# Forgetting attention: gate bias rows written to DRAM relative to each query block, instead of formed on GpSimd

## The chip, the cores and the metric

One Trainium2 chip, one of its cores. The metric is device time in microseconds, the median of several executions of one launch. The names of the engines in the profile: PE is TensorE's matmul, PEld its weight load, DVE is VectorE, ACT is ScalarE, POOL is GpSimd, SP is SyncE, which here only issues transfers.

## The reference, cut to what matters

The model has two layers over a residual stream of 512 positions by 1024 features. Layer 0 is a dilated-window attention with a gated ConvFFN. Layer 1 is the "forgetting attention" (FoX) with its own ConvFFN. Its keys, values and forget gates come from the stream after layer 0:

```python
kvf = rms_norm(h, kv_norm) @ w_kvf
k_sh = kvf[..., :B_WIDTH].reshape(B, T, B_HEADS, HEAD_DIM)
v_sh = kvf[..., B_WIDTH:2 * B_WIDTH].reshape(B, T, B_HEADS, HEAD_DIM)
log_f = jax.nn.log_sigmoid((kvf[..., 2 * B_WIDTH:] + b_f).astype(jnp.float32))
c_sh = jnp.cumsum(log_f, axis=1)
...
for i in range(T // BLK):            # fox_mixer; BLK = 128, T = 512, 16 heads of 64
    q0, q1 = i * BLK, (i + 1) * BLK
    s = jnp.einsum('bqhd,bkhd->bhqk', q[:, q0:q1], k[:, :q1]).astype(jnp.float32) * scale
    s = s + (c_t[:, :, q0:q1, None] - c_t[:, :, None, :q1])
    causal = jnp.arange(q0, q1)[:, None] >= jnp.arange(q1)[None, :]
    s = jnp.where(causal, s, NEG)
    p = jax.nn.softmax(s, axis=-1).astype(v.dtype)
    outs.append(jnp.einsum('bhqk,bkhd->bqhd', p, v[:, :q1]))
```

The bias of a score is the cumulative gate of the query minus that of the key. A term that is the same for all keys of one query drops out of the softmax. So the bias of a row may be taken against any fixed position: against the query itself, or against the first query of the block.

## The kernel before

All of it runs in float32 on one core. A matrix operand is split into a high part and a remainder, and a product is three matmuls (the helper `mm3`, L283 to L285). Weights arrive through the class `Weights`: a transfer on SyncE's queue brings a piece of 128 by 1024 (L50), ScalarE rounds it to the high part (`high`, L60), and VectorE subtracts to get the remainder (`low`, L78). For some pieces ScalarE writes the negative high part (`minus`, L71) and a transfer from GpSimd's queue adds the raw weight to it (`low_added`, L98). `ahead` and `ahead_dma` say how many pieces are prepared and loaded ahead. Loads, issues and engine instructions stand in each engine's queue in the order in which the source calls them (the schedule is manual). Waits follow from data and from buffers: a tile comes out of a pool and waits for the last use of what lay in its place. The pool `t4` has ten places of 4 KB in each partition; it holds raw weights, the bias tiles, the probabilities, gains and some of the tiles `dsums` (sums of down-projection weights for the next ConvFFN, formed on VectorE at L586 to L589 and written to DRAM from GpSimd's queue at L594).

The stage that the change edits begins after the ConvFFN of layer 0. First come the keys in eight chunks (`keys`, with the remainders at L1446). Beside them the generator `gates` forms the cumulative log gates `c8`, 16 heads by 512 positions, times 8 (L1480, L1481); times 8 because the scores are scaled by 1/8 together with the bias. At chunk 6 `c8` is written to DRAM as `cd` (L1576). After the keys TensorE transposes `c8` into `cq`, which has a column for each query block and head (L1579; copied out of PSUM at L1581). Then come the second half of the values, in four weight steps with the first query projections between them. `load_ck(j)` (L1531) loads the rows of the two heads of pair j from `cd`, repeated over all 128 partitions.

The attention loop runs over 32 units (j, i): head pair j = 0..7, query block i = 0..3, so unit (j, i) has (i + 1) x 128 keys. Its stages are a pipeline over the step n:

- `f_scores`: TensorE, scores of blocks 2 and 3 of pair j and of blocks 0 and 1 of pair j + 1, in the steps with i = 2 (L1630);
- `f_bias`: GpSimd, for unit n + 1 (L1612, L1613, see the diff);
- `f_exp`: VectorE adds scores and bias and takes the row minimum of the negated sum (L1640), ScalarE takes the exponential with its row sum (L1642), for unit n;
- `f_norm`: VectorE, reciprocal (L1650) and scaling of the probabilities in place, one instruction for each head (L1652), for unit n - 1;
- `f_transpose`: TensorE transposes the probabilities of unit n - 2 (L1664), ScalarE copies them out of PSUM (L1666);
- `f_pv`: TensorE, probabilities times values, four units at a time (L1679); `f_out_high` (L1689) and `f_out_low` (L1693) split the output.

Between these stand the query projections of the next pairs (`q_part`, six matmuls each, with `q_high` L1552 and `q_low` L1558) and the first part of the output projection (`acc`) near the end. The query projections run out in pair 6. Weight pieces are prepared in the same loop by `W.high`, `W.low`, `W.minus` and `W.low_added`.

Of the kernel before, what the change touches and what calls it, by code (L numbers as in the profile page):

```python
# [9 lines left out]
F32 = mybir.dt.float32  # L10
# [3 lines left out]
ALU = mybir.AluOpType  # L14

D = 1024
T = 512
# [6 lines left out]
NEG = -1e30  # L24
# [93 lines left out]
def trunk_kernel(ctx, tc, x, norm_gains, w_qkv_a, w_o_a, w_q_b, w_o_b, kv_norm, w_kvf, b_f,  # L118
                 w_up, conv_w, conv_b, w_down, rope, out):
    nc = tc.nc  # L120
    act, dve, pool, pe, sp = nc.scalar, nc.vector, nc.gpsimd, nc.tensor, nc.sync
# [5 lines left out]
    sml = ctx.enter_context(tc.tile_pool(name="sml", bufs=6))  # L127
    psp = ctx.enter_context(tc.tile_pool(name="psp", bufs=8, space=bass.MemoryType.PSUM))

    def t8(shape, dt=F32, name="t8"):  # L130
        return p8.tile(shape, dt, tag="t8", name=name)

    def t4(shape, dt=F32, name="t4"):
        return p4.tile(shape, dt, tag="t4", name=name)

    def t2(shape, dt=F32, name="t2"):
        return p2.tile(shape, dt, tag="t2", name=name)

    def bank(shape, name="bank"):
        return psp.tile(shape, F32, tag="ps", name=name)  # L140
# [114 lines left out]
    ident = cst.tile([128, 128], F32, name="ident")  # L255
# [15 lines left out]
    for s in range(2):  # L271
# [5 lines left out]
                       fill=NEG, base=0, channel_multiplier=-1)  # L277
    pool.affine_select(mask0[:, 128:256], mask0[:, 128:256], pattern=[[-1, 128]], compare_op=ALU.is_ge,
                       fill=NEG, base=0, channel_multiplier=1)
    same = cst.tile([128, 4], F32, name="same")  # L280

    def mm3(o, ah, al, bh, bl, first, last, shared=False):
        pe.matmul(o, ah, bh, start=first, stop=False, skip_group_check=shared)  # L283
        pe.matmul(o, ah, bl, start=False, stop=False, skip_group_check=shared)  # L284
        pe.matmul(o, al, bh, start=False, stop=last, skip_group_check=shared)  # L285
# [78 lines left out]
    def xs(xT, kc, s):  # L364
        return xT[0][kc // 4][:, kc % 4, s], xT[1][kc // 4][:, kc % 4, s]
# [1073 lines left out]
    def keys(c):  # L1439
        o = bank([128, T], name="k_ps")  # L1440
        feat_mm(W.get(), bd2.xT, o, ALL)
        if c % 2 == 0:
            kst[c // 2] = t8([128, 2, 2, T], F32R, name=f"kst{c // 2}")
        k = kst[c // 2][:, c % 2]
        act.copy(k[:, 0], o)
        dve.tensor_tensor(k[:, 1], o, k[:, 0].bitcast(F32), ALU.subtract)  # L1446

    c8 = t2([16, T], name="c8")
# [38 lines left out]
    def values(banks, w, s, blocks):  # L1487
        for b in blocks:
            for k in range(2):
                kc = 2 * s + k  # L1490
                ah, al = xs(bd2.xT, kc, slice(b * 128, b * 128 + 128))
                mm3(banks[b], ah, al, w[0][:, k, :], w[1][:, k, :], kc == 0, kc == KD - 1)

    def value_weight():
        return [t.rearrange("p (k c) -> p k c", k=2) for t in W.get()]

    def keep_values(hf, b, o):
        if hf not in Vt:
            Vt[hf] = t8([128, 4, 512], name=f"Vt{hf}")
        (act.copy if b % 2 else dve.tensor_copy)(Vt[hf][:, b, :], o)  # L1500
# [22 lines left out]
    del wv  # L1523
    next(down1)

    cks = {}

    def load_ck(j):
        t = t4([128, 2, T], name="ck")
        s = cd[2 * j:2 * j + 2, :]  # L1530
        sp.dma_start(t, bass.AP(tensor=s.tensor, offset=s.offset, ap=[[0, 128], [T, 2], [1, T]]))  # L1531
        cks[j] = t

    qT = {}
    qps = {}
# [1 line left out]
    def q_part(j, i):  # L1537

        if j >= 8:
            return  # L1540
        if i == 0:
            qps[j] = (bank([128, T], name="q_ps"), [t.rearrange("p (k c) -> p k c", k=8) for t in W.get()])
        o, (wh, wl) = qps[j]
        for kc in (2 * i, 2 * i + 1):
            bh, bl = xs(xTq, kc, ALL)
            mm3(o, wh[:, kc, :], wl[:, kc, :], bh, bl, kc == 0, kc == KD - 1)

    def q_high(j):
        if j >= 8:
            return  # L1550
        qT[j] = t8([128, 2, T], F32R, name="qst")
        act.copy(qT[j][:, 0], qps[j][0])  # L1552

    def q_low(j):
        if j >= 8:
            return
        o, t = qps.pop(j)[0], qT[j]
        dve.tensor_tensor(t[:, 1], o, t[:, 0].bitcast(F32), ALU.subtract)  # L1558

    cd = tc.dram_tile([16, T], F32, name="cd")  # L1560


    xTq = [], []
    for c in range(8):
        keys(c)
        for kc in range(2 * c, min(2 * c + 2, KD)):
            if kc % 4 == 0:
                for part, name in zip(xTq, ("xqh", "xql")):
                    part.append(t8([128, 4, T], F32R, name=f"{name}{kc // 4}"))
            bd2.second(xTq, kc)  # L1570
        if 1 <= c <= 5:
            next(gate)
        if c in (0, 1):
            next(down1)
        if c == 6:
            sp.dma_start(cd, c8)  # L1576
    cqp = bank([128, 4, 16], name="cq_ps")
    for b in range(4):
        pe.transpose(cqp[:, b, :], c8[:, b * 128:(b + 1) * 128], ident[:16, :16])  # L1579
    cq = sml.tile([128, 4, 16], F32, tag="cq", name="cq", bufs=1)  # L1580
    dve.tensor_copy(cq, cqp)  # L1581


    banks = [bank([128, 512], name="v_ps") for _ in range(4)]
    for s in range(4):
        values(banks, value_weight(), s, range(4))
        next(down1, None)
        if s == 0:
            W.ahead = 2
            q_part(0, 0)  # L1590
            q_part(0, 1)
            load_ck(0)
        elif s == 1:
            q_part(0, 2)
        elif s == 2:
            q_part(0, 3)
            q_high(0)
            q_low(0)
    for b in range(4):
        keep_values(1, b, banks[b])  # L1600


    prob = {}

    bia = {}

    def f_bias(j, i):
        n = (i + 1) * 128
        bias = t4([128, 2, T], name="bias")
        for hh in range(2):  # L1610
            hd = 2 * j + hh
            pool.tensor_scalar(bias[:, hh, :n], cks[j][:, hh, :n], -1.0, cq[:, i, hd:hd + 1], ALU.mult, ALU.add)  # L1612
        pool.affine_select(bias[:, :, n - 128:n], bias[:, :, n - 128:n], pattern=[[0, 2], [-1, 128]],  # L1613
                           compare_op=ALU.is_ge, fill=NEG, base=0, channel_multiplier=1)
        bia[j, i] = bias

    sc = {}

    def f_scores(j, blocks):
        wide = blocks[0] >= 2  # L1620
        if not wide:
            both = [bank([128, 2, 256], name="s_ps") for _ in range(2)]
        k = kst[j // 2][:, j % 2]
        for i in blocks:
            nn = max(256, (i + 1) * 128)
            sc[j, i] = [bank([128, T], name="s_ps") for _ in range(2)] if wide else [o[:, i] for o in both]
            for qp, kp in ((0, 0), (0, 1), (1, 0)):
                for hh in range(2):
                    own = slice(64 * hh, 64 * hh + 64)
                    pe.matmul(sc[j, i][hh][:, :nn], qT[j][own, qp, i * 128:(i + 1) * 128], k[own, kp, :nn],  # L1630
                              start=qp + kp == 0, stop=qp == 1)
# [63 lines left out]
    units = [(j, i) for j in range(8) for i in range(4)]  # L1695
    po = Proj(8, 4, lambda kc: (OTb[kc // 2][:, 0, kc % 2, :], OTb[kc // 2][:, 1, kc % 2, :]))
    wo = W.n_get + 7
    fill = [(kc, b) for b in range(2) for kc in range(4)]
    W.ahead, W.ahead_dma = 1, 1
    for i in range(3):  # L1700
        q_part(1, i)
        if i == 0:
            W.split(W.n_get + 1)
    f_bias(0, 0)
    N = len(units)
    pv_next = 0
    down1 = down_sums([(1, 9), (1, 10)], in_one, pool, 2, 0)
# [12 lines left out]
    for n in range(N + 3):  # L1720
        live = n < N
        if live:
            j, i = units[n]
            if i == 0 and j + 1 < 8:
                load_ck(j + 1)
            if i == 2:
                q_part(j + 2, 1)
                f_scores(j, (2, 3))
                if j + 1 < 8:
                    f_scores(j + 1, (0, 1))  # L1730
                values_of(n)
        if live:
            f_exp(j, i)
        if 1 <= n <= N:
            f_norm(*units[n - 1])
        if live:
            if n + 1 < N:
                f_bias(*units[n + 1])
            if i == 1:
                q_low(j + 1)  # L1740
            if i == 2 and j < 2 or (j, i) >= (6, 2):
                W.low()
            if i == 3 and j:
                f_out_low(j - 1)
            if i != 2:
                q_part(j + 1 + (i > 0), (i + 3) % 4)
            if (j, i) in ((7, 1), (7, 2)):
                next(down1)
        if 2 <= n < N + 2:
            f_transpose(*units[n - 2])  # L1750
        if live and i == 1 and 2 <= j < 6:
            W.minus()
            W.low_added()
        if n >= N + 3 - len(fill):
            po.both(*fill[n - N - 3 + len(fill)])

        if n >= N and n % 4 in (0, 2):
            values_of(n)
        while outs:
            f_out_high(outs.pop())  # L1760
        if live and i == 0:
            q_high(j + 1)
        if live and (i == (j < 2) if j < 6 else (j, i) >= (6, 1) and W.n_split < wo + 4):
            W.high()
# [53 lines left out]
```

## Time and profile before

| what | value |
|---|---|
| time, median of 3 (lowest to highest) | 1107.25 us (1107.01 to 1107.43) |
| time of the profiled execution | 1107.3 us |
| its span in the trace | 1105.5 us |
| busy: TensorE matmul, VectorE, ScalarE, GpSimd | 1095.3, 878.3, 672.3, 213.3 us |
| transfers: bytes, mean rate | 236.26 MB, 214 GB/s |
| GpSimd in the stretch 580 to 722 us: L1612 with 128, 256, 384, 512 keys | 16 each, mean 453, 650, 722, 915 ns |
| GpSimd there: L1613 | 32, mean 439 ns |

The span is the time from the first to the last instruction in the trace; the time of the execution has 1.8 us more around it. Rows of a timeline give the start in microseconds from the begin of the span, the duration (of a run of equal instructions: from the first start to the last end), engine, line, operation, output <- inputs, sizes and count; in brackets stands the idle time of the engine ahead of the row and what ended it. Matmuls overlap, so the duration of a row on TensorE is longer than the step to the next row; the starts are what to compare.

### The profile page before, as it was taken

The page shows a single profiled execution, that of the slowest core. Times are in us where ns is not written, and L with a number is a line of the kernel's source. Part 1 is how long each engine was busy: PE and PEld are TensorE (multiplying, and loading weights), DVE is VectorE, ACT ScalarE, POOL GpSimd, SP SyncE. Part 2 cuts the span into 40 slices and gives each one's busy share as a digit, 9 for nine tenths or more (in the row PEclk, how much of TensorE's full clock was granted, in tenths as well). Part 3 has the DMA queues.
Part 4 walks back from the last instruction along what each step waited for, and adds up shares of the span by engine and source line. Part 5 has one row for each costly group of instructions (what it writes and reads, how often), then busy time and mean ns, then how long its engine had stood idle before and what let it go on. Part 6 is the DMA issues. An engine that isn't in the chain of part 4 may idle for free.

```text
span 1105.5 us, 18058 instructions
## 1 busy us (share of the span) xinstructions
PE 1095.3 (99%) x6609; PEld 951.4 (86%) x6609; DVE 878.3 (79%) x1493; ACT 672.3 (61%) x1116; POOL 213.3 (19%) x309
## 2 busy tenths in 40 slices
PE   9999999999999999999999999999999999999997
PEld 6988889899999988888878788789899999988886
DVE  6697788888788689897686677868888788779894
ACT  7654575756666747576451587746656666647572
POOL 2632001311111211000000546500311111211000
PEclk9999999999999999999999999999999999999999
DMA  9799854477987989794447434684368878979862
GB/s 323 179 367 411 312 170 136 90 184 187 214 191 185 243 264 324 287 322 116 133 153 274 172 108 123 187 267 128 84 179 202 203 186 186 235 265 325 311 248 76
DMA packets 184928, 236.26 MB, mean 214 GB/s; under 512 B 12352, under 2 KB 132152, under 8 KB 184840
## 3 DMA queue, kind: packets, MB, share of 16 engines
q1 hardware_dynamic: 169224, 182.94, 50.9%
q0 software_dynamic: 14944, 52.18, 20.6%
q8 instruction: 52, 0.85, 0.3%
q14 instruction: 36, 0.29, 0.1%
q10 hardware_dynamic: 672, 0.00, 0.0%
HBM read 166.08 MB, written 39.63 MB: 186 GB/s over the span
## 4 chain that ended last, share of the span: by engine, by line
PE 94%; ACT 2%; DVE 1%; DMA 1%; issue 1%; POOL 0%; SPq 0%; DVEq 0%; ACTq 0%; POOLq 0%
PE up L284 13%; PE up L283 13%; PE up L285 13%; PE acc L283 9%; PE acc L285 8%; PE acc L284 8%; PE v_ps L283 2%; PE v_ps L285 2%; PE v_ps L284 2%; PE qk_ps L284 2%; PE qk_ps L283 2%; PE qk_ps L285 2%; PE first L285 1%; PE first L283 1%; PE first L284 1%; PE k_ps L285 1%
## 5 line engine op out<-in xcount | busy, mean ns | idle before, releaser
L283 PE MATMUL acc<-w 128*128 128x512 f32 (+1 forms) x311 | 120.6, 388 | 0.3 <-DVE mix L332 0.3
L285 PE MATMUL acc<-w 128*128 128x512 f32 (+1 forms) x311 | 120.4, 387 | 0.0
L284 PE MATMUL acc<-w 128*128 128x512 f32 (+1 forms) x267 | 103.2, 387 | 0.0
L283 PE MATMUL up<-xsh,w 128*128 128x256 f32 x352 | 99.6, 283 | 0.0
L284 PE MATMUL up<-xsl,w 128*128 128x256 f32 x352 | 99.6, 283 | 0.0
L285 PE MATMUL up<-xsh,w 128*128 128x256 f32 x352 | 99.6, 283 | 0.0
L78 DVE TENSOR_TENSOR w<-wraw,w 128x1024 fp32r<-128x1024 f32 x62 | 82.0, 1339 | 21.6 <-ACT w L60 21.2
L620 ACT ACTIVATE bb<-up,conv 128x512 f32<-128x512 f32 x80 | 59.6, 776 | 58.7 <-DVE up L1007 47.9
L60 ACT CAST w<-wraw 128x1024 fp32r<-128x1024 f32 x82 | 84.3, 1048 | 17.1 <-PE v_ps L284 6.9
L284 PE MATMUL up<-xcl,w 128*128 128x512 f32 (+1 forms) x276 | 93.5, 339 | 0.0
L284 PE MATMUL up<-xbl,w 128*128 128x512 f32 (+1 forms) x276 | 93.5, 339 | 0.0
L283 PE MATMUL up<-xbh,w 128*128 128x512 f32 (+1 forms) x276 | 93.5, 339 | 0.0
L283 PE MATMUL up<-xch,w 128*128 128x512 f32 (+1 forms) x276 | 93.5, 339 | 0.0
L285 PE MATMUL up<-xbh,w 128*128 128x512 f32 (+1 forms) x276 | 93.5, 339 | 0.0
L285 PE MATMUL up<-xch,w 128*128 128x512 f32 (+1 forms) x276 | 93.4, 338 | 0.0
L283 PEld LDWEIGHTS acc<-w 128*128 128x128 f32 x311 | 58.4, 188 | 12.4 <-DVE mix L332 0.7
L285 PEld LDWEIGHTS acc<-w 128*128 128x128 f32 x311 | 58.4, 188 | 12.0
L283 PEld LDWEIGHTS up<-xsh,w 128*128 128x128 f32 x352 | 67.6, 192 | 0.0
L284 PEld LDWEIGHTS up<-xsl,w 128*128 128x128 f32 x352 | 67.6, 192 | 0.0
L285 PEld LDWEIGHTS up<-xsh,w 128*128 128x128 f32 x352 | 67.6, 192 | 0.0
L621 DVE SCALAR_TENSOR_TENSOR bb<-up,conv,bb 128x511 f32<-128x511 f32 x80 | 59.5, 743 | 5.5 <-ACT bb L620 5.5
L623 DVE SCALAR_TENSOR_TENSOR bb<-up,conv,bb 128x510 f32<-128x510 f32 x80 | 59.9, 748 | 2.8
(312 smaller groups left out, 3154.8 us busy)
## 6 DMA issues: line engine op xcount, KB each, us to landing
wraw<-in_w_up_dram SPq DMA_DIRECT2D x88, 512.0 KB, 5.7
w<-wraw POOLq DMA_DIRECT2D x32, 512.0 KB, 6.4
dT<-dsums SPq DMA_DIRECT2D x28, 512.0 KB, 6.6
w<-wsum POOLq DMA_DIRECT2D x24, 512.0 KB, 5.8
dsums<-in_w_down_dram SPq DMA_DIRECT2D x22, 512.0 KB, 7.5
dsums<-in_w_down_dram SPq DMA_DIRECT2D x44, 256.0 KB, 7.5
hD<-hc POOLq DMA_DIRECT2D x44, 256.0 KB, 6.4
dact<-hD SPq DMA_DIRECT2D x44, 256.0 KB, 5.4
```

Source lines behind the costliest of these rows:

```text
L60: self.nc.scalar.copy(pair[:, 0], raw)
L78: self.nc.vector.tensor_tensor(pair[:, 1], raw, pair[:, 0].bitcast(F32), ALU.subtract)
L283: pe.matmul(o, ah, bh, start=first, stop=False, skip_group_check=shared)
L284: pe.matmul(o, ah, bl, start=False, stop=False, skip_group_check=shared)
L285: pe.matmul(o, al, bh, start=False, stop=last, skip_group_check=shared)
L620: act.activation(bb[:, s, :], ps, AF.Identity, bias=cp[:, 3, ch:ch + 1], scale=cp[:, 2, ch:ch + 1])
L621: dve.scalar_tensor_tensor(bb[:, s, 1:], ps[:, :T - 1], cp[:, 1, ch:ch + 1], bb[:, s, 1:], ALU.mult, ALU.add)
L623: dve.scalar_tensor_tensor(bb[:, s, 2:], ps[:, :T - 2], cp[:, 0, ch:ch + 1], bb[:, s, 2:], ALU.mult, ALU.add)
```

## The change

`cd` becomes four arrays of 16 by 512 in DRAM. Array i holds c of the first position of query block i minus c of every position, formed on VectorE as `rel` at key chunk 6, one instruction and one write for each block. The transposes of `c8` and the tile `cq` go. Instead of one load of `c` for each head pair there is one load for each unit, of the first (i + 1) x 128 keys of array i, straight into the unit's bias tile, issued three units ahead. GpSimd's two additions for each unit go; its mask over the last 128 columns (the diagonal block) stays, and now works on the loaded tile.

```diff
-    cks = {}
-
-    def load_ck(j):
-        t = t4([128, 2, T], name="ck")
-        s = cd[2 * j:2 * j + 2, :]
-        sp.dma_start(t, bass.AP(tensor=s.tensor, offset=s.offset, ap=[[0, 128], [T, 2], [1, T]]))
-        cks[j] = t
+    bia = {}
+
+    def load_bias(n):
+        j, i = divmod(n, 4)
+        if j < 8:
+            bia[j, i] = t = t4([128, 2, T], name="bias")
+            m = (i + 1) * 128
+            s = cd[i, 2 * j:2 * j + 2, :m]
+            sp.dma_start(t[:, :, :m], bass.AP(tensor=s.tensor, offset=s.offset, ap=[[0, 128], [T, 2], [1, m]]))
...
-    cd = tc.dram_tile([16, T], F32, name="cd")
+    cd = tc.dram_tile([4, 16, T], F32, name="cd")
...
         if c == 6:
-            sp.dma_start(cd, c8)
-    cqp = bank([128, 4, 16], name="cq_ps")
-    for b in range(4):
-        pe.transpose(cqp[:, b, :], c8[:, b * 128:(b + 1) * 128], ident[:16, :16])
-    cq = sml.tile([128, 4, 16], F32, tag="cq", name="cq", bufs=1)
-    dve.tensor_copy(cq, cqp)
+            for i in range(4):
+                rel = t2([16, T], name="rel")
+                dve.tensor_scalar(rel, c8, -1.0, c8[:, i * 128:i * 128 + 1], ALU.mult, ALU.add)
+                sp.dma_start(cd[i], rel)
...
-            load_ck(0)
+            load_bias(0)
         elif s == 1:
             q_part(0, 2)
+            load_bias(1)
         elif s == 2:
             q_part(0, 3)
             q_high(0)
             q_low(0)
+            load_bias(2)
...
-    def f_bias(j, i):
-        n = (i + 1) * 128
-        bias = t4([128, 2, T], name="bias")
-        for hh in range(2):
-            hd = 2 * j + hh
-            pool.tensor_scalar(bias[:, hh, :n], cks[j][:, hh, :n], -1.0, cq[:, i, hd:hd + 1], ALU.mult, ALU.add)
-        pool.affine_select(bias[:, :, n - 128:n], bias[:, :, n - 128:n], pattern=[[0, 2], [-1, 128]],
-                           compare_op=ALU.is_ge, fill=NEG, base=0, channel_multiplier=1)
-        bia[j, i] = bias
+    def f_mask(j, i):
+        d = bia[j, i][:, :, i * 128:(i + 1) * 128]
+        pool.affine_select(d, d, pattern=[[0, 2], [-1, 128]], compare_op=ALU.is_ge, fill=NEG, base=0,
+                           channel_multiplier=1)
...
-    f_bias(0, 0)
+    f_mask(0, 0)
...
             j, i = units[n]
-            if i == 0 and j + 1 < 8:
-                load_ck(j + 1)
+            load_bias(n + 3)
...
             if n + 1 < N:
-                f_bias(*units[n + 1])
+                f_mask(*units[n + 1])
```

More of the change, by code (lines that the diff above doesn't have):

```diff
@@ L1603, in trunk_kernel @@
     prob = {}
-    bia = {}
-    def f_bias(j, i):
-        n = (i + 1) * 128
-        bias = t4([128, 2, T], name="bias")
-        for hh in range(2):
-            hd = 2 * j + hh
-            pool.tensor_scalar(bias[:, hh, :n], cks[j][:, hh, :n], -1.0, cq[:, i, hd:hd + 1], ALU.mult, ALU.add)
-        pool.affine_select(bias[:, :, n - 128:n], bias[:, :, n - 128:n], pattern=[[0, 2], [-1, 128]],
-                           compare_op=ALU.is_ge, fill=NEG, base=0, channel_multiplier=1)
-        bia[j, i] = bias
+    def f_mask(j, i):
+        d = bia[j, i][:, :, i * 128:(i + 1) * 128]
+        pool.affine_select(d, d, pattern=[[0, 2], [-1, 128]], compare_op=ALU.is_ge, fill=NEG, base=0,
+                           channel_multiplier=1)
     sc = {}
```

## The prediction

> **What bounds the kernel now.** I read the page's busy times first, then TensorE's list of waits, then busy time by stretch over the attention stage that the change edits, then the timelines there, engine by engine.
>
> ```profile
> span 1105.5 us, 18058 instructions
> ...
> PE 1095.3 (99%) x6609; PEld 951.4 (86%) x6609; DVE 878.3 (79%) x1493; ACT 672.3 (61%) x1116; POOL 213.3 (19%) x309
> ```
> ```profile
> PE pT_ps L1664 <- DVE prob L1652: 1.4, 3, 1.1
> ```
> ```profile
> 690.00:700.00 10.00, 9.91 (x92) 7.95 (x90) 8.81 (x32) 8.15 (x23) 8.30 (x17) 1.00 0.79 207
> 700.00:710.00 10.00, 8.66 (x72) 6.83 (x68) 9.45 (x26) 7.66 (x22) 8.38 (x11) 1.00 0.76 264
> ```
>
> The columns of the last view are the stretch, its length, the busy time of TensorE (PE), its weight loads, VectorE (DVE), ScalarE (ACT) and GpSimd (POOL) with their instructions, the granted clock, the share of time in which the transfer engines were busy, and GB/s. TensorE is the bound at full clock (1.00), and its matrix work is not edited. So what the edit can give is what TensorE loses in or near this stage; what it can cost is a new TensorE wait. The list of waits has 1.4 us, but "busy" ends are modelled, so I measure losses by start times instead. First an undisturbed stretch, as a ruler:
>
> ```profile
> 645.18 0.82 PE L1664 MATMUL pT_ps<-ident,prob 128*128 128x128 f32 x6
> 645.76 0.48 PE L283 MATMUL q_ps<-xqh,w 128*128 128x512 f32 x1
> ...
> 647.00 0.39 PE L285 MATMUL q_ps<-xqh,w 128*128 128x512 f32 x1
> 647.23 1.04 PE L1664 MATMUL pT_ps<-ident,prob 128*128 128x128 f32 x8
> 648.02 0.47 PE L283 MATMUL q_ps<-xqh,w 128*128 128x512 f32 x1
> ...
> 649.58 2.21 PE L1630 MATMUL s_ps<-kst,qst 64*128 64x384 f32 x24
> 651.73 0.54 PE L1679 MATMUL o_ps<-pT,Vt 128*64 128x128 f32 x5
> ```
>
> A 512-wide matmul gives way to the next instruction after 0.23 us (647.00 to 647.23), 6 transposes take 0.58, 8 take 0.79 (0.105 per transpose more), 24 score matmuls 2.15. Three places fall behind this ruler; I call them A, B and C:
>
> ```profile
> 631.79 0.40 PE L285 MATMUL q_ps<-xqh,w 128*128 128x512 f32 x1
> 632.36 0.55 PE L1664 MATMUL pT_ps<-ident,prob 128*128 128x128 f32 x3 [0.17 <-DVE prob L1652]
> ...
> 633.39 0.47 PE L283 MATMUL q_ps<-xqh,w 128*128 128x512 f32 x1
> ```
> ```profile
> 694.69 2.14 PE L1664 MATMUL pT_ps<-ident,prob 128*128 128x128 f32 x14
> 696.76 2.62 PE L1630 MATMUL s_ps<-kst,qst 64*128 64x384 f32 x24
> 699.31 0.55 PE L1679 MATMUL o_ps<-pT,Vt 128*64 128x128 f32 x6
> ```
> ```profile
> 705.56 0.40 PE L285 MATMUL acc<-w,OTb 128*128 128x512 f32 x1
> 707.03 0.66 PE L1664 MATMUL pT_ps<-ident,prob 128*128 128x128 f32 x4 [1.07 <-DVE prob L1652]
> 707.96 0.63 PE L1664 MATMUL pT_ps<-ident,prob 128*128 128x128 f32 x4 [0.27 <-ACT pT L1666]
> 708.34 0.47 PE L283 MATMUL acc<-w,OTb 128*128 128x512 f32 x1
> ```
>
> A: 633.39 should have been 631.79 + 0.23 + 0.58 = 632.60, lost 0.79. B: 14 transposes should take 0.79 + 6 x 0.105 = 1.42, with 0.1 to the score matmuls and 2.15 for them, so 698.36 instead of 699.31, lost 0.95. C: 705.56 + 0.23 + 0.79 = 706.58 instead of 708.34, lost 1.76.
>
> **The change, part by part.**
>
> *The four transposes of c (L1579) go.*
>
> ```profile
> 589.00 0.39 PE L285 MATMUL k_ps<-xkh,w 128*128 128x512 f32 x1
> 589.32 0.41 PE L1579 MATMUL cq_ps<-ident,c 16*128 16x16 f32 x4
> ...
> 590.00 0.39 PE L284 MATMUL v_ps<-w,xkh 128*128 128x512 f32 x1
> ```
>
> From 589.00 to the second value matmul at 590.00 are 1.00 us; without the four it is two steps of 0.23. Gain 0.54, on the path itself.
>
> *GpSimd's 64 additions (L1612) go, its 32 masks (L1613) stay.*
>
> ```profile
> L1612 POOL TENSOR_SCALAR bias<-ck,cq x64: 368/688/1914, 618.2 to 707.5; 128x128 f32<-128x128 f32 x16, 128x256 f32<-128x256 f32 x16, 128x384 f32<-128x384 f32 x16, 128x512 f32<-128x512 f32 x16
> ...
> L1613 POOL TENSOR_SCALAR_AFFINE_SELECT bias<-bias x32: 407/408/1274, 619.0 to 709.5; 128x256 f32<-128x256 f32 x32
> ```
> ```profile
> 631.56 1.41 DVE L1652 TENSOR_SCALAR prob<-prob,rl 128x384 f32<-128x384 f32 x2
> ...
> 694.84 1.28 DVE L1652 TENSOR_SCALAR prob<-prob,rl 128x512 f32<-128x512 f32 x2
> ...
> 697.68 0.68 DVE L1558 TENSOR_TENSOR qst<-q_ps,qst 128x512 fp32r<-128x512 f32 x1
> ...
> 713.93 0.75 DVE L1652 TENSOR_SCALAR prob<-prob,rl 128x384 f32<-128x384 f32 x2
> ...
> 716.64 0.88 DVE L1652 TENSOR_SCALAR prob<-prob,rl 128x512 f32<-128x512 f32 x2
> ```
>
> The last two rows come after the last addition (707.5): there VectorE's normalisation of a pair takes 0.75 and 0.88. In A the same shape took 1.41, in B 1.28. I read the difference as VectorE held up by GpSimd. In A the second half would be done at 631.56 + 0.75 = 632.31 instead of 632.97, 0.66 earlier, and the last three transposes wait for just that half: of 0.79 I take 0.66. In B the normalisation would end 0.40 earlier, and the small one behind it and the query subtraction at 697.68, for which the second dozen of score matmuls waits, earlier still; I take 0.93 of 0.95. Bounds for each: 0, if the masks hold VectorE as long, and the whole loss.
>
> C is different:
>
> ```profile
> 705.71 1.06 ACT L60 CAST w<-wraw 128x1024 fp32r<-128x1024 f32 x1
> ...
> 707.43 0.85 ACT L1666 COPY pT<-pT_ps 128x384 f32<-128x384 f32 x2
> ```
>
> TensorE's last four transposes there start at 707.96, as ScalarE's copies end, and ScalarE ran a weight conversion and an exponential right up to those copies. GpSimd does not touch this. Bounds 0 and 1.76; I take 0.25, near the end that ScalarE's rows give.
>
> *Four VectorE rows (rel) and four writes to DRAM in place of one.* They have the shape of the scaling of c:
>
> ```profile
> 582.43 0.41 DVE L1481 TENSOR_SCALAR c<-c 16x512 f32<-16x512 f32 x1
> ...
> 590.04 0.69 DVE L1446 TENSOR_TENSOR kst<-k_ps,kst 128x512 fp32r<-128x512 f32 x1 [3.27 <-ACT kst L1445]
> ```
> ```profile
> 595.45 1.05 ACT L60 CAST w<-wraw 128x1024 fp32r<-128x1024 f32 x1 [4.49 <-PE v_ps L285]
> ```
>
> 4 x 0.41 = 1.64 us, ahead of VectorE's 3.27 us of idle time (586.77 to 590.04), which hides them; without that cover they would cost up to 1.64. The copy of cq (L1581) goes. On SyncE's queue the writes stand ahead of two value weights, dsums loads and a query weight. c was ready at 582.84; rel is ready at the latest by 586.77 + 1.64 = 588.4, so all of these leave up to 5.6 us later. The third value weight is converted at 595.45, and that conversion waited for TensorE to release a buffer, not for the load; I take 0, bound by a 1 us loss.
>
> *32 loads of bias rows in place of 8 of c.* Per head pair 128 partitions x 2 heads x 4 bytes x (128 + 256 + 384 + 512) = 1.31 MB instead of 0.52 MB. Each is issued three units ahead, and a unit lasts some 2.8 us (32 of them in the 618.2 to 707.5 of the L1612 row). Each waits in SyncE's queue for its buffer out of ten: for transposes or exponentials one to three units old. Queued behind are the weights of the next pairs, which in the kernel before waited for the same transposes and exponentials. GpSimd's masks wait for the loads; behind a mask in its queue stand the weight DMAs that accumulate (L98), and VectorE's score additions (L1640) wait for the mask. All this lies beside TensorE: 0, with the loss bounded by the last rival.
>
> Sum against the profiled execution (span 1105.5, time 1107.3): 0.54 + 0.66 + 0.93 + 0.25 = 2.38, so 1104.9. The median, 1107.25, is 0.05 lower, which changes nothing.
>
> **The rivals.**
>
> *The masks hold VectorE too.* For it: 32 masks of 0.41 us stay, one per unit, and the loads free GpSimd to run each early, against any VectorE instruction. Against: a unit has one mask of 0.41 where it had two additions of 0.69 besides. A and B would each give 0.41 less (gain 1.56), or nothing, with C, if each half meets a mask (gain 0.54): 1105.7 to 1106.8. The Trainium skill, page SBUF — State Buffer, section Who interferes with whom, states this as a rule: the second port pair of VectorE is shared with GpSimd and is an exclusive lock, held for the whole instruction by whoever starts first. By that rule the masks still lock; A's 1.41 against 0.75 is what it looks like here.
>
> *C goes too.* For it: its first wait, 1.07, is put down to the stretched normalisation, and VectorE was 9.45 of 10 us busy in that stretch. Against: the copies above. With 1.07 to 1.76 for C in place of 0.25 the gain is 3.2 to 3.9: 1103.4 to 1104.1.
>
> *A weight comes late (slower).*
>
> ```profile
> wraw<-in_w_o_b_dram SPq DMA_DIRECT2D x8, 512.0 KB, 6.2
> ```
> ```profile
> 694.81 6.75 SPq L50 DMA_DIRECT2D wraw<-in_w_o_b_dram  x3
> ```
> ```profile
> 702.87 1.06 ACT L60 CAST w<-wraw 128x1024 fp32r<-128x1024 f32 x1
> ```
>
> In head pair 6 no query projections are left to fill TensorE. The output weight issued at 694.81 is converted on ScalarE at 702.87, 8.06 us later, and landing takes 6.2; ScalarE sets C's end, so a weight later than 8.1 us costs TensorE one for one. The transfer engines are 0.79 busy there, and the bias rows of pairs 6 and 7 now share them. From 8.06 + 2.38 = 10.4 us on the gain is gone; with one weight 5 us late it is 1104.9 + 5 = 1109.9, with two 3 us late each 1110.9. Against it: only 0.13 to 0.4 MB more stands ahead of each weight.
>
> **How the numbers follow.** Forecast 0.50 (own range 1104.3 to 1105.4), masks 0.17, C too 0.20, late weight 0.13. A measurement of this kernel tells some 0.2% (2.2 us) from no change, so the line is at 1105.04: two thirds of the forecast's chance lie below it, all of "C too", none of "masks". Faster 0.33 + 0.20 = 0.53, same 0.17 + 0.17 = 0.34, slower 0.13. The range takes in C too and the masks with the 0.54 alone, and a part of the 1 us by which the third value weight was bounded: 1103.3 to 1107.2; what is left out is most of the late weight's 0.13.
>
> **What would show it.** Value matmuls should follow the key matmuls 0.23 us apart. The longest L1652 pair should fall from 1.28 to 1.41 towards 0.75 to 0.88. A and B should be gone by start times, and C should still start its last transposes as ScalarE's copies end. TensorE should have no wait put down to a bias load or a weight. The forecast is wrong if the stretched pairs stay stretched, if the stage shortens by over 3 us, or if a conversion on ScalarE waits for its load.

## The result and the profile after

| what | before | after |
|---|---|---|
| time, median (lowest to highest), side by side, 14 runs each | 1107.74 us (1106.92 to 1109.31) | 1105.17 us (1104.58 to 1106.94) |
| ratio after to before, 95% interval | | 0.998 (0.9973 to 0.9988) |
| time of the profiled execution, its span | 1107.3, 1105.5 us | 1104.97, 1102.9 us |
| last key matmul to the transposes of the convolution's rows (L566), starts | 136.54 us | 133.84 us |

The change takes 2.57 us from the median, 0.2%. The last row of the table is a ruler for the whole edited stage: it leaves out what differs upstream (the last key matmul starts at 589.00 before and at 589.24 after, with the same TensorE instructions ahead of it). It loses 2.70 us, in one execution of each kernel.

The page of the kernel after, its busy times; then the stretch from 700 to 710 us in the columns of the prediction; then TensorE's list of waits (what waited, for what, us in total, times, longest):

```profile
span 1102.9 us, 18083 instructions
...
PE 1094.1 (99%) x6605; PEld 951.6 (86%) x6605; DVE 873.1 (79%) x1496; ACT 671.5 (61%) x1116; POOL 173.0 (16%) x245
```
```profile
700.00:710.00 10.00, 9.19 (x70) 7.10 (x70) 9.34 (x31) 9.19 (x24) 2.14 (x3) 1.00 0.86 300
```
```profile
PE pT_ps L1659 <- DVE prob L1647: 0.8, 1, 0.8
```

GpSimd is busy 40 us less, VectorE 5; in the stretch of C GpSimd works 2.14 of 10 us in place of 8.38, and the transfer engines 0.86 in place of 0.76. Of TensorE's waits for the normalisation (1.4 in 3 before) one is left, in C. The line numbers have moved by five: the transposes are L1659, the normalisation L1647, the scores L1625, the mask L1609. The same places by start times, kernel after, timeline of TensorE; first the way from keys to values and the end of the ruler:

```profile
589.24 0.39 PE L285 MATMUL k_ps<-xkh,w 128*128 128x512 f32 x1
589.47 0.39 PE L283 MATMUL v_ps<-w,xkh 128*128 128x512 f32 x1
589.70 0.39 PE L284 MATMUL v_ps<-w,xkh 128*128 128x512 f32 x1
...
723.08 0.44 PE L566 MATMUL cv_ps<-ident,cv_rows 44*128 44x44 f32 x4
```

Keys give way to values in two steps of 0.23: 0.46 in place of 1.00. Then A, B and C:

```profile
631.45 0.40 PE L285 MATMUL q_ps<-xqh,w 128*128 128x512 f32 x1
631.70 0.94 PE L1659 MATMUL pT_ps<-ident,prob 128*128 128x128 f32 x6
632.39 0.48 PE L283 MATMUL q_ps<-xqh,w 128*128 128x512 f32 x1
...
693.70 1.69 PE L1659 MATMUL pT_ps<-ident,prob 128*128 128x128 f32 x14
695.32 2.21 PE L1625 MATMUL s_ps<-kst,qst 64*128 64x384 f32 x24
697.46 2.40 PE L1674 MATMUL o_ps<-pT,Vt 128*64 128x128 f32 x40
...
703.80 0.40 PE L285 MATMUL acc<-w,OTb 128*128 128x512 f32 x1
705.01 1.11 PE L1659 MATMUL pT_ps<-ident,prob 128*128 128x128 f32 x8 [0.81 <-DVE prob L1647]
705.88 0.47 PE L283 MATMUL acc<-w,OTb 128*128 128x512 f32 x1
```

By the prediction's ruler A loses 632.39 - 631.45 - 0.81 = 0.13 (0.79 before), B 697.46 - 693.70 - 3.67 = 0.09 (0.95 before), C 705.88 - 703.80 - 1.02 = 1.06 (1.76 before). The gains are 0.66, 0.86 and 0.70; with 0.54 for the transposes of c that is 2.76, against 2.70 by the whole stretch.

Now the instruction that was meant to be held up, first in the kernel before, then after (one line's view: shortest, median and longest in ns, first and last start):

```profile
L1652 DVE TENSOR_SCALAR prob<-prob,rl x64: 280/484/2034, 623.7 to 717.0; 128x128 f32<-128x128 f32 x16, 128x256 f32<-128x256 f32 x16, 128x384 f32<-128x384 f32 x16, 128x512 f32<-128x512 f32 x16
```
```profile
L1647 DVE TENSOR_SCALAR prob<-prob,rl x64: 273/415/505, 623.8 to 714.6; 128x128 f32<-128x128 f32 x16, 128x256 f32<-128x256 f32 x16, 128x384 f32<-128x384 f32 x16, 128x512 f32<-128x512 f32 x16
```
```profile
L1609 POOL TENSOR_SCALAR_AFFINE_SELECT bias<-bias x32: 396/722/1480, 618.4 to 707.2; 128x256 f32<-128x256 f32 x32
```

The longest normalisation falls from 2.03 to 0.51 us. In A the pair took 1.41 and in B 1.28; in the kernel after the same two rows are

```profile
631.22 0.75 DVE L1647 TENSOR_SCALAR prob<-prob,rl 128x384 f32<-128x384 f32 x2
...
693.16 0.88 DVE L1647 TENSOR_SCALAR prob<-prob,rl 128x512 f32<-128x512 f32 x2
```

The median of the masks goes the other way, from 0.41 before to 0.72. That is not one mask taking longer: sixteen of the 32 now run in four groups of four, each behind an adding weight transfer in GpSimd's queue. The rows within a group overlap, and a whole group takes 1.79. Single masks still take 0.41, except a few that ran beside VectorE's weight subtraction; GpSimd's rows, then VectorE's:

```profile
676.19 1.79 POOL L1609 TENSOR_SCALAR_AFFINE_SELECT bias<-bias 128x256 f32<-128x256 f32 x4
...
702.17 1.43 POOL L1609 TENSOR_SCALAR_AFFINE_SELECT bias<-bias 128x256 f32<-128x256 f32 x1 [1.87 <-DVE prob L1647]
```
```profile
702.11 1.22 DVE L78 TENSOR_TENSOR w<-wraw,w 128x1024 fp32r<-128x1024 f32 x1
```

B has a second part, which the prediction did not count. VectorE's row at the head of B, before and after, and GpSimd's row before:

```profile
691.39 0.69 DVE L1640 CUSTOM_DVE_ANT_0 prob<-s_ps,bias 128x512 f32<-128x512 f32 x1 [1.05 <-POOL bias L1613]
```
```profile
688.97 0.69 DVE L1635 CUSTOM_DVE_ANT_0 prob<-s_ps,bias 128x512 f32<-128x512 f32 x1 [0.28 <-POOL bias L1609]
```
```profile
689.19 1.69 POOL L1612 TENSOR_SCALAR bias<-ck,cq 128x512 f32<-128x512 f32 x2
```

Before, VectorE waited 1.05 us there for a mask that stood behind two additions in GpSimd's queue; after, it waits 0.28. From 691.39 on VectorE was busy without a gap until the query subtraction that B waits for, so this late start counts in B beside the stretched normalisations. In A there is no such difference: VectorE's work starts 4.47 us ahead of the query matmul (627.32 to 631.79 before, 626.98 to 631.45 after) in both.

### The profile page after: what moved, and what is told of

The parts are those of the page before. It is cut to its first block, busy times and chain, and to the rows that moved or that the text cites. A ratio compares the mean times of both kernels' runs of the same rounds, so it can differ in the third digit from the quotient of the medians.

```text
span 1102.9 us, 18083 instructions
## 1 busy us (share of the span) xinstructions
PE 1094.1 (99%) x6605; PEld 951.6 (86%) x6605; DVE 873.1 (79%) x1496; ACT 671.5 (61%) x1116; POOL 173.0 (16%) x245
## 4 chain that ended last, share of the span: by engine, by line
PE 97%; DVE 1%; DMA 1%; issue 1%; ACT 0%; DVEq 0%
PE up L285 12%; PE up L284 12%; PE up L283 12%; PE acc L283 9%; PE acc L284 8%; PE acc L285 8%; PE v_ps L285 2%; PE v_ps L283 2%; PE v_ps L284 2%; PE qk_ps L284 2%; PE qk_ps L283 2%; PE qk_ps L285 2%; PE o_ps L1674 2%; PE pT_ps L1659 2%; PE s_ps L1625 2%; PE first L285 1%
```

## The experiments

All times are medians; the ratio is to the kernel before in runs beside it. "Stretch" is the ruler of the table above; A, B, C are us lost by starts in the profiled execution; the last column is the longest single normalisation. Medians that differ by less than 1 us can't be told apart here (every interval is some 2 us wide), so the small terms are read from the starts. These come from one execution of each kernel: low_later lost 0.78 us more than the changed kernel in A and B together, ahead of anything that it moves, so a stretch or a letter alone is no surer than that where no row shows the reason.

| kernel | time, us | ratio (95%) | stretch | A | B | C | longest, us |
|---|---|---|---|---|---|---|---|
| before | 1107.74 | | 136.54 | 0.79 | 0.95 | 1.76 | 2.03 |
| after | 1105.17 | 0.998 (0.9973 to 0.9988) | 133.84 | 0.13 | 0.09 | 1.06 | 0.51 |
| after_again | 1105.21 | 0.9979 (0.9970 to 0.9988) | 134.00 | 0.16 | 0.09 | 1.00 | 0.60 |
| adds_back | 1106.25 | 0.9985 (0.9977 to 0.9994) | 135.68 | 0.95 | 0.61 | 1.65 | 1.37 |
| old_no_gpsimd | 1105.08 | 0.9978 (0.9969 to 0.9986) | 134.48 | 0.03 | 0.16 | 1.22 | 0.49 |
| no_masks_b | 1105.11 | 0.9977 (0.9968 to 0.9987) | 133.82 | 0.03 | 0.09 | 1.16 | 0.49 |
| cq_back | 1105.56 | 0.9978 (0.9969 to 0.9986) | 134.62 | 0.12 | 0.09 | 1.00 | 0.64 |
| norm_first | 1104.80 | 0.9972 (0.9961 to 0.9982) | 133.74 | 0.11 | 0.09 | 0.78 | 0.52 |
| low_later | 1105.39 | 0.9977 (0.9967 to 0.9987) | 135.04 | 0.36 | 0.64 | 1.36 | 0.59 |
| pool_low | 1105.06 | 0.9981 (0.9972 to 0.9990) | 134.18 | 0.12 | 0.09 | 1.25 | 1.74 |
| lead1 | 1104.63 | 0.9971 (0.9959 to 0.9982) | 134.15 | 0.35 | 0.09 | 1.15 | 0.58 |
| rel16 | 1105.41 | 0.9975 (0.9965 to 0.9985) | 134.05 | 0.22 | 0.09 | 0.99 | 0.56 |

### GpSimd's additions, without their data (adds_back)

```diff
     def f_mask(j, i):
+        n = (i + 1) * 128
+        for hh in range(2):
+            pool.tensor_scalar(h[:, i, :n], h[:, i, :n], -1.0, 0.0, ALU.mult, ALU.add)
         d = bia[j, i][:, :, i * 128:(i + 1) * 128]
```

> The changed kernel with 64 additions on GpSimd of the old shapes, two ahead of each mask, on a tile that nothing in the attention reads (its sign is turned twice, so it stays what it was). Theory 1, GpSimd's additions hold VectorE's normalisation whatever they compute: the pairs of the normalisation stretch again (a single one over 1 us, where the changed kernel's longest is 0.505), TensorE loses a part or all of the 2.2 us that A, B and C gave back (0.66 + 0.86 + 0.70), and the run is 0.7 to 2.2 us longer than the changed kernel. Theory 2, the old loss came from VectorE waiting for the additions' result: nobody waits for these, so the normalisation stays at or below 0.505 us and the time is that of the changed kernel within 0.3 us.

The normalisation's line in this kernel, then TensorE in A, B and C, then VectorE in C:

```profile
L1650 DVE TENSOR_SCALAR prob<-prob,rl x64: 275/482/1373, 623.4 to 716.0; 128x128 f32<-128x128 f32 x16, 128x256 f32<-128x256 f32 x16, 128x384 f32<-128x384 f32 x16, 128x512 f32<-128x512 f32 x16
```
```profile
631.76 0.55 PE L1662 MATMUL pT_ps<-ident,prob 128*128 128x128 f32 x3 [0.30 <-DVE prob L1650]
632.54 0.52 PE L1662 MATMUL pT_ps<-ident,prob 128*128 128x128 f32 x3 [0.24 <-DVE prob L1650]
...
694.12 2.15 PE L1662 MATMUL pT_ps<-ident,prob 128*128 128x128 f32 x14
696.20 2.26 PE L1628 MATMUL s_ps<-kst,qst 64*128 64x384 f32 x24
...
706.44 1.11 PE L1662 MATMUL pT_ps<-ident,prob 128*128 128x128 f32 x8 [1.40 <-DVE prob L1650]
```
```profile
703.11 1.66 DVE L78 TENSOR_TENSOR w<-wraw,w 128x1024 fp32r<-128x1024 f32 x1 [0.31 <-ACT w L60]
...
705.90 0.88 DVE L1650 TENSOR_SCALAR prob<-prob,rl 128x512 f32<-128x512 f32 x2
```

Theory 1. No instruction of the attention needs the result of these additions, and still the normalisation has its old median (482 ns against 484), A breaks into two groups of three as before, B's fourteen transposes need 2.08 up to the scores in place of 1.62, and A, B and C together lose 3.21 us, 1.93 more than the changed kernel and near the 3.50 of the kernel before. The stretch is 1.84 longer, the median 1.1 (0.8 if each is taken against the kernel before beside it), with intervals that overlap. It is GpSimd's being at work that costs, not the result of its additions. But the three places don't lose in the same way. In A it is the normalisation (a pair of 1.11 and one of 1.07 ahead of it). In C the pair that TensorE waits for takes 0.88, as in the changed kernel; held is the weight subtraction ahead of it, 1.66 in place of 1.22, beside an addition pair that GpSimd ran from 703.08 to 705.25. In B VectorE waits 0.95 for a mask, which stands behind these additions too, so this kernel does not tell the held normalisation from the late mask.

### GpSimd left out altogether (old_no_gpsimd)

```diff
     def f_bias(j, i):
-        n = (i + 1) * 128
-        bias = t4([128, 2, T], name="bias")
-        for hh in range(2):
-            hd = 2 * j + hh
-            pool.tensor_scalar(bias[:, hh, :n], cks[j][:, hh, :n], -1.0, cq[:, i, hd:hd + 1], ALU.mult, ALU.add)
-        pool.affine_select(bias[:, :, n - 128:n], bias[:, :, n - 128:n], pattern=[[0, 2], [-1, 128]],
-                           compare_op=ALU.is_ge, fill=NEG, base=0, channel_multiplier=1)
-        bia[j, i] = bias
+        bia[j, i] = cks[j]
```

> The kernel before with GpSimd's 64 additions and 32 masks left out: scores get the row of c itself as bias, without mask. Loads, the write and the transposes of c stay as before. Theory 1, A, B and a part of C were GpSimd's alone: they fall to what the changed kernel has (0.13, 0.09, 1.06), 2.2 us less, and the transposes still take 1.00; stretch from the last key matmul to the transposes of the convolution's rows 136.5 - 2.2 = 134.3; time 1.9 to 2.5 below the kernel before and 0.3 to 0.7 above the changed one. Theory 2, the changed kernel's loads cost something that its gains hide: this one comes out at or below the changed kernel in spite of its transposes.

The stretch is 134.48, 2.06 below the kernel before, and the way from keys to values takes 1.00 as there. So 2.06 of the 2.70 us belong to GpSimd's work; 0.54 more are the transposes, and what is left, 0.10, is within the 0.16 by which two executions of the changed kernel differ. Theory 2 finds no support in the stretch. By the median alone (2.88 below the kernel before beside it, and 0.1 below the changed kernel's) theory 2's sign is met: it is lower than theory 1 allowed and doesn't show the 0.5 us that the transposes cost here. Medians don't resolve that, and the stretch is one execution, so the loads' cost is shown to be small and not to be nothing.

### The masks (no_masks, no_masks_b)

```diff
     def f_mask(j, i):
-        d = bia[j, i][:, :, i * 128:(i + 1) * 128]
-        pool.affine_select(d, d, pattern=[[0, 2], [-1, 128]], compare_op=ALU.is_ge, fill=NEG, base=0,
-                           channel_multiplier=1)
+        pass
```

> The changed kernel without GpSimd's 32 masks: the attention sees later positions of its diagonal block too. Theory 1 (the forecast), the masks cost TensorE nothing: A (0.13 lost), B (0.09) and C (1.06) stay within 0.15 each, the normalisations keep their 0.42 us median, time within 0.3 us of the changed kernel. Theory 2 (rival of the prediction), the masks still hold VectorE: C falls by 0.3 to 0.8 and the time by 0.5 to 1.0.

> The changed kernel without GpSimd's 32 masks, once more for its trace: the attention sees later positions of its diagonal block too. Theory 1, the masks cost TensorE nothing: A (0.13), B (0.09) and C (1.06) stay within 0.15 each and the stretch from the last key matmul to the transposes of the convolution's rows stays at 133.8. Theory 2, masks still hold VectorE or come late: the stretch falls by 0.5 to 1.0.

The first of the two had a median of 1104.69 us, ratio 0.9977 (0.9967 to 0.9986); the starts are read from the second. There the stretch is 133.82, against 133.84 and 134.00 with masks; A is 0.03, and C at 1.16 is no better. Theory 1: one mask for each unit costs TensorE nothing that the starts can show, apart from 0.1 in A.

### The transposes of c (cq_back)

```diff
+    cqp = bank([128, 4, 16], name="cq_ps")
+    for b in range(4):
+        pe.transpose(cqp[:, b, :], c8[:, b * 128:(b + 1) * 128], ident[:16, :16])
+    cq = sml.tile([128, 4, 16], F32, tag="cq", name="cq", bufs=1)
+    dve.tensor_copy(cq, cqp)
     banks = [bank([128, 512], name="v_ps") for _ in range(4)]
```

> The changed kernel with the four transposes of c and their copy on VectorE put back between key and value projection; nothing uses their result. Theory 1, they lie on TensorE's path alone: from the last key matmul to the second value matmul 1.00 us again instead of 0.46, everything behind it 0.54 later, time +0.5. Theory 2, the stage behind has slack that takes them up: the start of the transposed stage behind the attention (value of L566) moves by less than 0.2. Theory 3, the additional copy and bank cost VectorE or PSUM more: over 0.8.

TensorE between keys and values in this kernel:

```profile
588.91 0.39 PE L285 MATMUL k_ps<-xkh,w 128*128 128x512 f32 x1
589.23 0.41 PE L1586 MATMUL cq_ps<-ident,c 16*128 16x16 f32 x4
589.57 0.50 PE L283 MATMUL v_ps<-w,xkh 128*128 128x512 f32 x1
589.90 0.39 PE L284 MATMUL v_ps<-w,xkh 128*128 128x512 f32 x1
```

0.99 in place of 0.46, and the stretch is longer by 0.62 to 0.78. They lie on the path; A, B and C stay as they are. The median, 0.4 above the changed kernel (0.1 if each is taken against the kernel before beside it), can't prove it.

### What holds C (norm_first, low_later, pool_low)

In norm_first VectorE normalises unit (6,3) before it adds bias and scores of (7,0).

```diff
+        if n == 28:
+            f_norm(*units[n - 1])
         if live:
             f_exp(j, i)
-        if 1 <= n <= N:
+        if 1 <= n <= N and n != 28:
             f_norm(*units[n - 1])
```

> The changed kernel with one thing moved: at the first unit of pair 7 VectorE normalises (6,3) before it adds bias and scores of (7,0). Theory 1, what is left of C (1.06 us) is VectorE's order: the pair of 512 wide normalisations that began at 704.46 follows the 0.68 us subtraction directly, 0.6 earlier; TensorE's eight transposes start 0.4 to 0.6 earlier, C falls to 0.5 to 0.65, time -0.4 to -0.6 us. Theory 2 (the prediction's step), ScalarE holds C: no gain, C stays at 1.0 or over, and since ScalarE's exponential of (7,0) starts up to 0.6 later the time may grow by as much.

In low_later the low half of pair 5's output goes behind these additions too.

```diff
         if live:
             f_exp(j, i)
+        if n == 28:
+            f_out_low(5)
...
-            if i == 3 and j:
+            if i == 3 and j and n != 27:
                 f_out_low(j - 1)
```

> The changed kernel with the normalisation of (6,3) ahead of the additions of (7,0), as in norm_first, and besides the low half of pair 5's output (0.68 us on VectorE) moved from unit (6,3) to unit (7,0), behind these additions. Theory 1, C is set by VectorE's order: the pair of normalisations starts as ScalarE's exponential ends, 0.6 to 0.8 earlier than in norm_first; C falls from 0.78 there to 0.1 to 0.3, ScalarE's copies of pT are no longer late, and the stretch from the last key matmul to the transposes of the convolution's rows falls from 133.7 to 132.8 to 133.1 us; time 0.7 to 1.1 below the changed kernel. Theory 2, ScalarE holds the rest: C stays at 0.6 or more, no gain over norm_first.

In pool_low GpSimd does VectorE's one weight subtraction of unit (6,3).

```diff
+    def low_pool(self):
+        raw, pair = self.half_done.pop()
+        for q in range(2):
+            s = slice(512 * q, 512 * q + 512)
+            self.nc.gpsimd.tensor_tensor(pair[:, 1, s], raw[:, s], pair[:, 0, s].bitcast(F32), ALU.subtract)
+        self.ready[self.n_split] = (pair[:, 0], pair[:, 1])
+        self.n_split += 1
...
+            if n == 27:
+                W.low_pool()
-            if i == 2 and j < 2 or (j, i) >= (6, 2):
+            elif i == 2 and j < 2 or (j, i) >= (6, 2):
                 W.low()
```

> The changed kernel with the one weight subtraction that VectorE does in unit (6,3) (1.22 us, ahead of the normalisation that sets C) given to GpSimd as two subtractions of 512 columns, some 1.3 us each by the 5.1 us of its 2048 wide addition. Theory 1, GpSimd holds VectorE's normalisation whenever it works beside it: VectorE's queue is 1.2 us shorter, but the 512 wide normalisations of (6,3), now ready as ScalarE's exponential ends, fall into GpSimd's 2.6 us and stretch from 0.88 to 1.3 to 2.0; C stays between 0.8 and 1.6 and the time within 0.5 of the changed kernel. Theory 2, only many additions in a row hold it: the pair stays at 0.88, starts 0.5 earlier, C falls to 0.3 to 0.6 and the time by 0.5 to 0.8.

First VectorE and ScalarE in C: one row of VectorE in the kernel before, then one of each in the kernel after.

```profile
706.32 1.49 DVE L1652 TENSOR_SCALAR prob<-prob,rl 128x512 f32<-128x512 f32 x2
```
```profile
704.46 0.88 DVE L1647 TENSOR_SCALAR prob<-prob,rl 128x512 f32<-128x512 f32 x2
```
```profile
705.58 0.85 ACT L1661 COPY pT<-pT_ps 128x384 f32<-128x384 f32 x2
```

The pair that C waits for took 1.49 before and takes 0.88 after: 0.61 of C's 0.70. In the kernel after, TensorE's eight transposes run in one go from 705.01, the last four from about 705.44 (four of eight steps that fill 0.87), while ScalarE's copies begin at 705.58. So they don't wait for those copies, and the prediction's sign that they would still start as the copies end did not come. norm_first, VectorE and TensorE:

```profile
703.77 0.88 DVE L1647 TENSOR_SCALAR prob<-prob,rl 128x512 f32<-128x512 f32 x2
```
```profile
704.31 1.11 PE L1659 MATMUL pT_ps<-ident,prob 128*128 128x128 f32 x8 [0.54 <-DVE prob L1647]
705.18 0.47 PE L283 MATMUL acc<-w,OTb 128*128 128x512 f32 x1
...
706.74 1.50 PE L1625 MATMUL s_ps<-kst,qst 64*128 64x384 f32 x12
708.30 2.40 PE L1674 MATMUL o_ps<-pT,Vt 128*64 128x128 f32 x40
```

C falls by 0.28 to 0.78, half of what theory 1 said, and is still VectorE's. But from the scores to the product with the values it is now 1.56 (706.74 to 708.30; in the kernel after 1.42), probably since ScalarE's exponential of (7,0) and the copies behind it come later. The stretch of 133.74 is no gain that can be told from 133.84. low_later in C, TensorE:

```profile
706.17 0.66 PE L1659 MATMUL pT_ps<-ident,prob 128*128 128x128 f32 x4 [0.70 <-DVE OTb L1688]
```

Neither theory foresaw this. The instruction that I moved back also frees pair 5's bank in PSUM, and the last four transposes now wait for that bank: 0.70. C is 1.36, worse than without the move. This execution lost 0.64 in B too, ahead of anything that was moved; there VectorE had waited for the mask, as its own row and GpSimd's rows of the weight transfer and the masks show:

```profile
689.92 0.69 DVE L1635 CUSTOM_DVE_ANT_0 prob<-s_ps,bias 128x512 f32<-128x512 f32 x1 [1.69 <-POOL bias L1609]
```
```profile
688.58 0.88 POOL L98 DMA_DIRECT2D w<-wraw  x1 [10.39 <-ACT w L71]
689.16 1.79 POOL L1609 TENSOR_SCALAR_AFFINE_SELECT bias<-bias 128x256 f32<-128x256 f32 x4
```

The masks stand in GpSimd's queue behind an adding weight transfer that waited 10.39 us for ScalarE. No single normalisation in this kernel takes over 0.59, so this loss isn't the hold; what the rows show in its place is the late mask. pool_low, VectorE and GpSimd in C:

```profile
703.14 0.17 DVE L1653 RECIPROCAL rl<-ls 128x2 f32<-128x2 f32 x1 [0.37 <-ACT prob L1645]
703.34 1.80 DVE L1655 TENSOR_SCALAR prob<-prob,rl 128x512 f32<-128x512 f32 x2
```
```profile
701.78 2.54 POOL L77 TENSOR_TENSOR w<-wraw,w 128x512 fp32r<-128x512 f32 x2 [6.28 <-ACT w L60]
```

Theory 1 for the pair, and the plainest picture of the mechanism: VectorE's pair starts as soon as ScalarE allows and takes 1.80 in place of 0.88. GpSimd's subtractions end at 701.78 + 2.54 = 704.32, and 704.32 + 0.88 = 705.20, where the pair ends at 705.14: VectorE did next to nothing until GpSimd was done. The relief of 1.22 us on VectorE is eaten up; C is 1.25.

The Trainium skill, page SBUF — State Buffer, section Who interferes with whom, says that a VectorE instruction in a mode that uses both of its ports and a GpSimd instruction shut each other out: the second one to issue is blocked until the first is finished. These rows agree with that: the pair starts at 703.34, during GpSimd's subtractions, and ends as if it had begun when they ended.

### The loads and the rows (lead1, rel16)

```diff
-            load_bias(1)
...
-            load_bias(2)
...
-            load_bias(n + 3)
+            load_bias(n + 1)
```

> The changed kernel with each load of bias rows issued one unit ahead instead of three. Theory 1, the lead of three hides the loads and one of 2.8 us does not: the mask of each unit waits for its load, GpSimd's idle time put down to the load rises from 22 us to 40 or more, VectorE's additions wait for masks 10 us or more in sum instead of 3.7, and TensorE, two units behind, loses 1 to 10 us. Theory 2, the loads land within one unit: time within 0.5 us of the changed kernel.

```diff
                 sp.dma_start(cd[i], rel)
+            more = t2([16, T], name="more")
+            for i in range(12):
+                dve.tensor_scalar(more, c8, -1.0, c8[:, :1], ALU.mult, ALU.add)
```

> The changed kernel with twelve more rows of rel's shape on VectorE behind the four, nothing uses them: 12 x 0.41 = 4.9 us, while VectorE's idle time there, before the last subtraction of the key stage, is 2.05 us. Theory 1, the four rows are hidden and the cover is those 2 us plus what the weights have in hand: the twelve push the last key subtraction and the value weight behind them 2.9 us later; TensorE waits for a value weight by 0 to 2.9 us. Theory 2, VectorE has no cover there at all: all 4.9 us come back in the time, and then the four rows cost 1.6 us in the changed kernel too.

In lead1 GpSimd's idle time put down to the loads doubles; the view of the bias tile (idle time in us, times) has

```profile
  DMA bias<-cd: 44.6, 13
...
  POOL bias L1607: 4.0, 7
```

where the kernel after has 22.2 in 9 and 3.7 in 5. VectorE waits for masks no longer than that, and TensorE has no wait put down to a mask or a load: theory 2 in the time, though GpSimd's wait is the one that theory 1 named. A loses 0.2 more, but low_later, whose loads are those of the changed kernel, lost as much there; the stretch of 134.15 is 0.3 above the changed kernel's. A lead of one unit can't be told from one of three. In rel16, VectorE:

```profile
587.16 6.08 DVE L1584 TENSOR_SCALAR more<-c 16x512 f32<-16x512 f32 x12
...
594.30 0.67 DVE L1446 TENSOR_TENSOR kst<-k_ps,kst 128x512 fp32r<-128x512 f32 x1
```

Twelve more rows take 6.08 us, the last key subtraction comes some 4 us later (594.30; 590.29 in the kernel after), and the stretch is 134.05: nothing. The four rows were hidden with room to spare, more than theory 1 counted.

### The changed kernel once more (after_again)

> The changed kernel itself, as a second look at how far one execution's trace differs from another's. If A, B and C are set by program order alone, they come out at 0.13, 0.09 and 1.06 again, each within 0.1. If they hang on when loads land and masks run, one of them differs by 0.2 or more while the time stays within 0.1%.

A, B and C come out within 0.06 of the first execution's and the stretch within 0.16. low_later shows that an execution can do worse in B where masks come late.

None of these kernels can be told from the changed one as faster; lead1 and norm_first have the lowest medians, 0.4 to 0.5 below it, with intervals that overlap.

## Why the prediction was right, point by point

The forecast was 1104.9, the time 1105.17. The mechanism was the predicted one in the main, and one term was off. That the sum comes within 0.2 us of the 2.57 by the medians is in part luck: C's term was 0.45 too small, and single times of one kernel lie over 2 us apart.

- **Transposes of c**: predicted 0.54, measured 0.54 in the changed kernel, and back in cq_back.
- **A**: predicted 0.66, measured 0.66. **B**: predicted 0.93, measured 0.86. adds_back puts A and most of B back without any use of the additions' result, and old_no_gpsimd takes both away without any of the change's loads; that GpSimd's work costs TensorE these times is shown from both sides. In A the cause is the predicted one, the held normalisation. In B the number is right and the mechanism is half of it: the prediction counted the stretched normalisations and not the 1.05 us for which VectorE had waited for a mask behind the additions. How B's 0.86 divides between the two is not shown.
- **C**: predicted 0.25, measured 0.70. This is the term that was mis-sized, and its reason was wrong: "ScalarE's copies end" as TensorE's last four transposes start, "GpSimd does not touch this". The row named ScalarE as the releaser (0.27). But the second half of the stretched pair ended at 706.32 + 1.49 = 707.81, 0.15 ahead of those transposes' start at 707.96; VectorE explains them as well. low_later shows whose bank those four take: pair 5's. ScalarE had read it from 702.39 to 702.98 (L1689), long before. With the pair at 0.88, ScalarE no longer appears in C. The step that failed was to take the copy that the profile named without asking whether its buffer was the one needed.
- **rel, writes, loads at nothing**: right as far as the starts show. rel16 shows that the rows have more cover than I counted, and lead1 that the loads need less lead. That waits for masks lie beside TensorE holds in the changed kernel, where the one in B is 0.28; it need not hold in every execution, as low_later shows, where VectorE waited 1.69 for a mask and B lost 0.64. The transfer engines are busier in C (0.86), without a wait of TensorE for them.
- **Masks hold VectorE too**: not in a way that costs TensorE. The longest normalisation is 0.51 with the masks and 0.49 without them, and taking them out gives no time.
- **C goes too**: half. Its price began at 1.07 for C; 0.61 of the pair's stretch went, and 1.06 stays, since VectorE's queue in pair 6 is full: a weight subtraction of 1.22 and an output subtraction of 0.68 stand ahead of the pair. What would take the rest stays open: moving the pair ahead of the additions of (7,0) gave 0.28 and lost some of it again, two other moves made C worse.
- **A weight comes late**: didn't happen. No wait of TensorE is put down to a weight or a bias load in this stage; what it would take to make one late was not tried.

The sum was 2.38 and the stretch shows 2.70. The 0.45 that C gave over its term, less 0.07 that B gave under it, is 0.38, and 0.06 of the four gains isn't in the stretch.

## What to carry to other kernels

Before crediting a GpSimd helper with being free because it is 19% busy, compare the same VectorE instruction in stretches with and without GpSimd beside it: 0.75 against 1.41 us told the mechanism in advance. Ask too who waits for what stands behind the helper's work in its queue, as VectorE did for the mask in B. What such a removal is worth is then only what TensorE lost where it waited for VectorE, here 2 us, where GpSimd is busy 40 us less and VectorE 5. A releaser that the profile names is a candidate: check that the instruction named is the one whose result or buffer is needed, and look for a second one that ends within 0.2 us of it.

## What was not expected of the hardware

The hold works in both directions: a mask that takes 0.41 alone took 1.43 at 702.17 in the kernel after, where it came just behind the start of VectorE's weight subtraction (702.11, 1.22), and in adds_back such a subtraction took 1.66 beside GpSimd's additions. VectorE's additions of scores from PSUM and bias have a longest of 0.692 us before and 0.693 after, for 512 columns: that form isn't held by GpSimd's additions, where the normalisation in the same queue took up to 2.03. The Trainium skill, page SBUF — State Buffer, section Who interferes with whom, says that a VectorE instruction with at most one input in SBUF, outside the modes that use both ports, does not contend with GpSimd, and these two figures agree.
